# A one-core hybrid encoder step: the last group's value tiles get a pool of their own

## The chip, the cores and the metric

The kernel runs on one core of a Trainium2 chip. The metric is the device time of one execution in microseconds (us); of several runs the median counts. Engines are named as in the profile: PE is TensorE, the matrix engine (PEld are its weight loads), DVE is VectorE, ACT is ScalarE, POOL is GpSimd, SP is SyncE, which here issues the DMAs. L450 means line 450 of the kernel before.

## The reference

One inference step of a single layer, for a prompt of 1024 frames and, beside it, 32 frames of a running stream. All numbers are float32.

```python
proj = xn @ w_in                       # xn: normalised frames, (1056, 1024); w_in: 1024 columns of
                                       # queries and keys and more, then values and output gates
q, k, v, log_a -> o_a, s_gla           # gated linear attention, 6 heads, per-key decay
q, k, v, log_f -> o_b, s_hg            # HGRN2, 5 heads
q, k, v, log_f, ig -> o_c, (C, n, m)   # stabilised mLSTM, 5 heads, after a causal convolution
o = head_rms_norm(o) * gate            # for each of the three
x = x + rms_norm(concat(o_a, o_b, o_c) @ w_out)
up = causal_dwconv(rms_norm(x) @ w_up)
x = x + rms_norm((gelu(gate_half) * value_half) @ w_down)
```

The lines are shortened; the recurrences run in blocks of 64 frames, and the final states are outputs too.

## The kernel before, in words

The frames are cut into nine units: 0 to 7 are 128 prompt frames each, unit 8 is the 32 running frames. The in-projection works on three groups of units: 0 to 2, 3 to 5, and 6, 7 with 8 (288 frames). Its products are float32 built from three products of split operands: every operand x is kept as a rounded part xh and a rest xl, and a helper (`mm3`, L99 to L102) issues the three matmuls. Splitting costs a cast on ACT (sometimes on DVE) and a subtraction on DVE or POOL.

For each group the in-projection first makes the projections that feed queries, keys and gates (tiles `pf`), with their convolutions, exponentials and cumulative sums in the pool `pf`; the results go to DRAM (`qkb_d`, `mqk_d` and others) and are read back by the mixers. The last of them are four convolutions (`conv`, tiles pc, y, th, mo), whose results mo are stored to `mqk_d` and `mqks_d`. Then come eight blocks of 256 columns of values and output gates. In the first two groups, and for block 0, frames are the rows of the result. In the last group blocks 1 to 7 are computed the other way round (`vg_across`, L438): for each half e of a block, 24 matmuls put 128 columns by 288 frames into a PSUM buffer pv, ACT copies that into half of a tile vf (L456), and PE transposes vf back, unit by unit, into another PSUM buffer pb (`back`, L440 to L445). The transposes of a block are issued behind the matmuls of the next. From pb a value block goes through one ACT copy into a tile vg and out to DRAM; a gate block (blocks 4 to 7) goes through a tanh on ACT into a tile vth, of which there is one buffer, one or two DVE operations, and a product on POOL into vg (L408 to L424). Those PSUM buffers pv and pb, the transposes ctp and the products zp of the out-projection all have the tag "big" with three buffers.

The mixers (the three recurrences) are a generator per unit, 17 steps each, run in the order 0 to 5, then 8, 6, 7. They are traced between the steps of the in-projection of the next group and of the out-projection (`merge`, L1429).

The out-projection (`outproj`, L992) runs over the units 0, 1, 2, 3, 8, 4, 5, then 6 and 7. For a unit it loads the mixed frames ct from DRAM, transposes them on PE (ctp), splits them into ch (ACT, L1019) and cl (DVE, L1020), and multiplies with the eight slices of the split weights woh and wol, in two halves of 512 columns (zp). The weights are read from DRAM raw, slice by slice, into a ring of seven buffers wor that later holds ct, xr and z too (L664 to L669); slice 6 and 7 need a buffer that has been given back. `out_weights` (L979) splits the slices: the first two with ACT (L106) and DVE (L109), the others behind ch and cl of unit 0 (L986, L988).

On-chip memory is taken in pools that stack up from two sides. On the right, p1 holds the in-projection's tiles: x with the tag "x" (three buffers of 4 KB a partition, shared by the input frames and, in the last group, vf), gx, raw and split weights (tags wr, wh, wl), xh, xl, jk. p1 is closed after the three groups (L1455), and p2 (woh, wol, gm, ch, cl, oss) and p3 (x0, called xg in the profile) are opened in its place. On the left, above the mixers' pool mx, lies pf; in the last group it is closed after the convolutions, and pw, the ring of weights, is opened in its place (L662 to L664).

No order of the engines' instructions is written out here. A planner simulates a timeline and puts the instructions of each engine in order by priority, which follows the order of the trace except where `high_priority` or `issue_after` says otherwise. Waits between engines follow from the tiles' uses and from the pools. A pool that lands on a closed pool's bytes waits, by the default setting, for the users of that closed pool.

Of the kernel before, what the change touches and what calls it, by code (L numbers as in the profile page):

```python
# [8 lines left out]
F32 = mybir.dt.float32  # L9
# [81 lines left out]
def body(ctx: ExitStack, tc: tile.TileContext, a: dict):  # L91
# [7 lines left out]
    def mm3(ps, lh, rh, first, last, **kw):  # L99
        pe.matmul(ps, lh[0], rh[0], start=first, stop=False, **kw)  # L100
        pe.matmul(ps, lh[0], rh[1], start=False, stop=False, **kw)  # L101
        return pe.matmul(ps, lh[1], rh[0], start=False, stop=last, **kw)  # L102
# [21 lines left out]
    p1 = p1s.enter_context(tc.tile_pool(name="p1", bufs=1, side="right"))  # L124
# [127 lines left out]
    cols_of, dcs_of = {}, {}  # L252
    HSET = (2, 0, 4, 5)
    VGD = (lambda b, h: b > 0, lambda b, h: True, lambda b, h: True)
    pws, wo_raw, ring = ExitStack(), [], []
    NRING, CT0 = 7, 6

    ct_of, xr_of, tail, xlate, mixed = {}, {}, [], {}, set()
# [2 lines left out]
    def load_cat(u):  # L261
        if u in ct_of:
            return
        while u not in mixed:
            pump(1)
        n = 128 if u < 8 else DEC
        ct_of[u] = ring[0](f"ct{u}")
        sp.dma_start(ct_of[u][:n], cat_d[128 * u:128 * u + n, :])
# [8 lines left out]
    def units_of(g):  # L277
        t0, pl, sl = GROUPS[g]
        us = [(t0 // 128 + i, 128 * i, 128) for i in range(pl // 128)]
        if sl:  # L280
            us.append((8, pl, sl))
        return us
# [69 lines left out]
    def inproj(g, xh, xl, normed, scaled=None):  # L352
        t0, pl, sl = GROUPS[g]
        T = pl + sl
# [43 lines left out]
        def vg_weights(blk):  # L398
            parts = [(a["w_tok0"][:, ks[0]:ks[-1] + 1], ks, lt0_d[:, ks[0]:ks[-1] + 1]) for ks in VG0] if not blk else \
                [(a["w_tok"][blk - 1, hf], range(4 * hf, 4 * hf + 4), lt_d[blk - 1, hf]) for hf in range(2)]  # L400
            ws = []
            for i, (src, ks, low) in enumerate(parts):
                wh, wl, _ = weights(src, p1, f"wt{g}_{blk}_{i}", [128, len(ks), 256 if blk else 282],
                                    raw=wraw.pop((blk, i), None), eng=dve if VGD[g](blk, i) else pool, low=low, kept=g > 0)
                ws += [(wh[:, k], wl[:, k]) for k in range(len(ks))]
            return ws

        def vg_store(blk, u, off, n, ps):  # L408
            o = mx.tile([128, 256], F32, tag="vg", name=f"vg{u}_{blk}", bufs=3)
            t = t0 + off  # L410
            if blk < 4:
                act.copy(o[:n], ps[:n, :256])
                sp.dma_start(v_d[t:t + n, 256 * blk:256 * blk + 256], o[:n])
                return
            c0 = 256 * (blk - 4)
            th = mx.tile([128, 256], F32, tag="vth", name=f"vth{u}_{blk}", bufs=1)
            tanh(th[:n], ps[:n, :256], 0.5)
            ns = min(max(704 - c0, 0), 256)
            if ns:
                dve.scalar_tensor_tensor(th[:n, :ns], th[:n, :ns], 1.0, ps[:n, :ns], op0=ALU.add, op1=ALU.mult)  # L420
            if ns < 256:
                dve.tensor_scalar(th[:n, ns:], th[:n, ns:], 1.0, None, op0=ALU.add)
            pool.tensor_tensor(o[:n], th[:n], gh[:n, c0:c0 + 256], op=ALU.mult)
            sp.dma_start(g_d[t:t + n, c0:c0 + 256], o[:n])  # L424
# [13 lines left out]
        def vg_across(blks):  # L438

            def back(blk, fs, part):  # L440
                for (u, off, n) in units_of(g)[part]:
                    ps = psb.tile([128, 256], F32, tag="big", name=f"pb{u}_{blk}")
                    for e in range(2):
                        pe.transpose(ps[:n, 128 * e:128 * e + 128], fs[e][:, off:off + n], ident)
                    vg_store(blk, u, off, n, ps)  # L445

            before = None
            for blk in blks:
                ws = vg_weights(blk)
                fs = p1.tile([128, 2, T], F32, tag="x", name=f"vf{blk}", bufs=3)  # L450
                fs = [fs[:, 0], fs[:, 1]]
                for e in range(2):
                    ps = psb.tile([128, T], F32, tag="big", name=f"pv{g}_{blk}_{e}")
                    for k in range(8):
                        mm3(ps, [w[:, 128 * e:128 * e + 128] for w in ws[k]], (xh[:, k, :], xl[:, k, :]), k == 0, k == 7)
                    act.copy(fs[e], ps)  # L456
                    if before:
                        back(*before, slice(e, 1 + 2 * e))
                    yield
                before = (blk, fs)  # L460
                yield
            for e in range(2):
                back(*before, slice(e, 1 + 2 * e))
# [197 lines left out]
        if g == 2:  # L661
            pfs.close()  # L662
            pw = pws.enter_context(tc.tile_pool(name="pw", bufs=1, side="left"))
            ring.append(lambda name: pw.tile([128, 1024], F32, tag="ring", name=name, bufs=NRING))  # L664
            for k in range(8):
                if k == CT0:
                    load_cat(0)
                wo_raw.append(ring[0](f"wor{k}"))
                sp.dma_start(wo_raw[k], a["w_out"][k])  # L669
        if sl:  # L670
            yield from vg_across(range(1, 8))
            return
# [746 lines left out]
    side = []  # L1419
# [17 lines left out]
    def mixers(g):  # L1437
        us = [(u, 2 * i) for i, (u, off, n) in enumerate(units_of(g))]
        return chain_of(*[mixer(u, g, c) for (u, c) in us[-1:] + us[:-1]]) if us[-1][0] == 8 else \
            chain_of(*[mixer(u, g, c) for (u, c) in us])  # L1440
# [3 lines left out]
    for g in range(3):  # L1444
        xs_ = norm_tiles(g)
        n_side = (0, 3 * NMIX - 6, 3 * NMIX)[g]
        scaled = scale_x(0) if g == 0 else None
        if scaled:
            next(scaled)
            next(scaled)  # L1450
        merge(inproj(g, *xs_, norm_group(g, *xs_), scaled), NIN, n_side)
        if g == 0:
            mixer_zeros()
        side.append(mixers(g))
    p1s.close()  # L1455
    p2s = ExitStack()
    p2 = p2s.enter_context(tc.tile_pool(name="p2", bufs=1, side="right"))
    wo = outproj_setup(p2)
# [42 lines left out]
    blk = up_block(pw_, 0, 0, W0, X[0], uus[0], own)  # L1501
# [184 lines left out]
```

## Time and profile before

| what | us |
|---|---|
| median of 3 runs | 1431.09 |
| lowest and highest of them | 1427.78 and 1431.60 |
| profiled execution, its own time | 1433.42 |
| its span, first to last instruction | 1431.6 |
| PE busy in the span | 1375.1 (96%) |
| DVE busy | 1006.9 (70%) |
| ACT busy | 710.2 (50%) |
| POOL busy | 273.5 (19%) |

The times of instructions are counted from the span's start. A row of the timeline gives start, duration, engine, line, operation, the tiles written and read, shapes and the number of merged instructions; in brackets stands how long the engine was idle before it and what ended that. A row of waits names who waited for whom, then the total, the number and the longest. A row of the chain gives start, share on the chain, and the instruction. Matmuls are pipelined, so the durations of neighbours overlap.

In this execution the last group's value blocks run from 438.7 to 525.8, the out-projection's products zp from 536.0 to 701, and the feed-forward part fills the rest.

### The profile page before, as it was taken

The numbers are of one execution on the slowest core, as the hardware profiler recorded it, in microseconds if no ns is written. First come the engines' busy times: TensorE is split into PE (matmuls) and PEld (weight loads), VectorE is DVE, ScalarE is ACT, GpSimd is POOL, SyncE is SP. The second block draws the span as 40 slices with busy tenths as digits, with TensorE's granted clock in tenths as the row PEclk, the third lists the DMA queues.
The fourth block names the chain that finished last, engine by engine and source line by source line (L and its number), as shares of the span: only waits on it lengthen the run. The fifth ranks groups of instructions, "written<-read, shape, count | busy, mean of one in ns | idle before, by whom it ended". The sixth has DMA issues, their size and how long they took to land.

```text
span 1431.6 us, 30048 instructions
## 1 busy us (share of the span) xinstructions
PE 1375.1 (96%) x11804; PEld 1258.5 (88%) x11804; DVE 1006.9 (70%) x1827; ACT 710.2 (50%) x1403; POOL 273.5 (19%) x456
## 2 busy tenths in 40 slices
PE   7989999999998999899989999999999999999998
PEld 6989889898887887767789999999999999988886
DVE  5796468846597669685888887887888875653644
ACT  5545456535474546243665454554555455543432
POOL 6531111213021244132221111111111110000100
PEclk9999999999999999999999999999999999999999
DMA  9599778766789845352412222222222257775752
GB/s 345 189 317 355 229 244 298 236 228 210 262 248 303 313 124 188 122 178 60 162 54 91 85 82 91 75 78 73 91 75 75 76 183 235 227 230 180 238 180 99
DMA packets 132438, 255.11 MB, mean 178 GB/s; under 512 B 28648, under 2 KB 79368, under 8 KB 132296
## 3 DMA queue, kind: packets, MB, share of 16 engines
q1 hardware_dynamic: 132295, 253.19, 53.3%
q8 instruction: 92, 1.51, 0.4%
q14 instruction: 51, 0.41, 0.1%
HBM read 192.26 MB, written 60.89 MB: 177 GB/s over the span
## 4 chain that ended last, share of the span: by engine, by line
PE 71%; DVE 11%; DMA 8%; ACT 5%; issue 3%; POOL 2%; SPq 1%; DVEq 0%; POOLq 0%; ACTq 0%
PE pd L102 6%; PE pd L101 6%; PE pd L100 6%; PE pux L102 4%; PE pux L100 4%; PE pux L101 4%; PE pv L102 3%; PE pv L100 3%; PE pv L101 3%; PE puw L100 3%; PE puw L101 3%; PE puw L102 3%; DMA qkb<-qkb_d 2%; PE zp L100 2%; PE zp L101 2%
## 5 line engine op out<-in xcount | busy, mean ns | idle before, releaser
L1260 DVE SCALAR_TENSOR_TENSOR y<-uu,fconv_sb,y 128x1060 f32<-128x1060 f32 x88 | 116.3, 1321 | 28.3 <-ACT y L1258 27.5
L102 PE MATMUL pd<-wd,hl 128*128 128x512 f32 x264 | 105.1, 399 | 0.0
L101 PE MATMUL pd<-wd,hh 128*128 128x512 f32 x264 | 104.2, 395 | 0.0
L100 PE MATMUL pd<-wd,hh 128*128 128x512 f32 x264 | 103.5, 393 | 0.0
L1254 POOL COPY uu<-uu 128x2 f32<-128x2 f32 x44 | 35.3, 802 | 210.0 <-DVE uu L1202 209.9
L1197 ACT COPY c<-pux 128x274 f32<-128x274 f32 (+1 forms) x132 | 48.9, 375 | 41.2 <-PE pux L102 38.3
L1258 ACT ACTIVATE y<-uu,fconv_sb 128x1060 f32<-128x1060 f32 x44 | 56.0, 1273 | 21.1 <-POOL uu L1255 20.6
L100 PE MATMUL zp<-woh,ch 128*128 128x512 f32 (+1 forms) x144 | 58.8, 415 | 3.9 <-DVE cl L1020 2.9
L101 PEld LDWEIGHTS pd<-wd,hh 128*128 128x128 f32 x264 | 49.6, 188 | 12.5
L100 PEld LDWEIGHTS pd<-wd,hh 128*128 128x128 f32 x264 | 49.6, 188 | 11.7
L102 PEld LDWEIGHTS pd<-wd,hl 128*128 128x128 f32 x264 | 49.6, 188 | 11.4
L100 PE MATMUL pv<-wt_0h,xh 128*128 128x256 f32 (+2 forms) x195 | 57.8, 297 | 1.7 <-ACT xh L316 1.7
L101 PE MATMUL zp<-wol,ch 128*128 128x512 f32 (+1 forms) x144 | 58.8, 408 | 0.0
L102 PE MATMUL zp<-woh,cl 128*128 128x512 f32 (+1 forms) x144 | 58.2, 408 | 0.2 <-DVE cl L1020 0.2
L102 PE MATMUL pv<-wt_1h,xl 128*128 128x256 f32 (+2 forms) x195 | 57.4, 294 | 0.5 <-DVE xl L317 0.5
L102 PE MATMUL pv<-wt_0h,xl 128*128 128x256 f32 (+2 forms) x195 | 57.1, 293 | 0.6 <-DVE xl L317 0.6
L101 PE MATMUL pv<-wt_1l,xh 128*128 128x256 f32 (+2 forms) x195 | 56.9, 292 | 0.0
L100 PE MATMUL pv<-wt_1h,xh 128*128 128x256 f32 (+2 forms) x195 | 56.9, 292 | 0.0
L101 PE MATMUL pv<-wt_0l,xh 128*128 128x256 f32 (+2 forms) x195 | 56.8, 291 | 0.1
L100 PE MATMUL pd<-hh,wd 128*128 128x288 f32 x176 | 52.1, 297 | 0.0
L101 PE MATMUL pd<-hl,wd 128*128 128x288 f32 x176 | 52.1, 296 | 0.0
L218 POOL TENSOR_SCALAR hrs<-hss 128x5 f32<-128x5 f32 (+3 forms) x27 | 14.5, 537 | 196.4 <-DVE hss L888 195.8
(1675 smaller groups left out, 5179.5 us busy)
## 6 DMA issues: line engine op xcount, KB each, us to landing
h_d<-y SPq DMA_DIRECT2D x22, 530.0 KB, 3.3
wt_0r<-in_w_tok SPq DMA_DIRECT2D x21, 512.0 KB, 5.5
wt_1r<-in_w_tok SPq DMA_DIRECT2D x21, 512.0 KB, 5.9
wt_0l<-lt_d SPq DMA_DIRECT2D x14, 512.0 KB, 4.5
wt_1l<-lt_d SPq DMA_DIRECT2D x14, 512.0 KB, 5.6
qkb<-qkb_d SPq DMA_DIRECT2D x8, 768.0 KB, 6.4
hr<-h_d SPq DMA_DIRECT2D x44, 128.0 KB, 3.3
hr<-h_d SPq DMA_DIRECT2D x22, 192.0 KB, 4.1
```

The source lines that it names most:

```text
L100: pe.matmul(ps, lh[0], rh[0], start=first, stop=False, **kw)
L101: pe.matmul(ps, lh[0], rh[1], start=False, stop=False, **kw)
L102: return pe.matmul(ps, lh[1], rh[0], start=False, stop=last, **kw)
L218: pool.tensor_scalar(out, ss, 1.0 / width, EPS, op0=ALU.mult, op1=ALU.add)
L1197: kept[name] = act.copy(t, ps)
L1254: pool.tensor_copy(u[:, GAP_P:GAP_P + 2], u[:, GAP_S - 2:GAP_S])
L1258: act.activation(y, u, AF.Identity, scale=fconv[:, j, 2:3], bias=fconv[:, j, 3:4])
L1260: dve.scalar_tensor_tensor(y, uu[i][:, s:s + NCOL], fconv[:, j, s:s + 1], y, op0=ALU.mult, op1=ALU.add)
```

## The change

The tiles vf leave the tag "x" of p1. They get a pool of their own, pvf, with three buffers of 2,304 bytes a partition, opened on the left right after pw (so above it, on bytes that pf had) and closed right after p1, before p2 is opened. Everything else, each instruction and each DMA, is the same.

```diff
@@ body
-    pws, wo_raw, ring = ExitStack(), [], []
+    pws, pvs, wo_raw, ring, vfs = ExitStack(), ExitStack(), [], [], []
@@ vg_across
                 ws = vg_weights(blk)
-                fs = p1.tile([128, 2, T], F32, tag="x", name=f"vf{blk}", bufs=3)
+                fs = vfs[0].tile([128, 2, T], F32, tag="vf", name=f"vf{blk}", bufs=3)
                 fs = [fs[:, 0], fs[:, 1]]
@@ inproj
         if g == 2:
             pfs.close()
             pw = pws.enter_context(tc.tile_pool(name="pw", bufs=1, side="left"))
+
+            vfs.append(pvs.enter_context(tc.tile_pool(name="pvf", bufs=1, side="left")))
             ring.append(lambda name: pw.tile([128, 1024], F32, tag="ring", name=name, bufs=NRING))
@@ body, after the three groups
     p1s.close()
+    pvs.close()
     p2s = ExitStack()
```

## The prediction

> **What bounds the kernel now.** I read the page first, then the busy time by stretches, then the waits on the two tiles that the change separates, then the timeline at both ends of their life. The page gives the frame:
>
> ```profile
> span 1431.6 us, 30048 instructions
> PE 1375.1 (96%) x11804; PEld 1258.5 (88%) x11804; DVE 1006.9 (70%) x1827; ACT 710.2 (50%) x1403; POOL 273.5 (19%) x456
> ```
>
> PE (TensorE) is busy for 96% of the span, so a change can only win where PE idles or runs slowly. The next view gives, for each stretch, busy time and count of PE, weight loads, DVE, ACT and POOL, then the granted clock, the DMA share and GB/s.
>
> ```profile
> 456.00:460.00 4.00, 2.29 (x18) 2.04 (x16) 2.63 (x6) 3.01 (x9) 0.00 (x0) 1.00 0.87 317
> 460.00:464.00 4.00, 2.42 (x13) 2.43 (x14) 3.80 (x12) 1.82 (x4) 0.00 (x0) 0.79 1.01 399
> 464.00:526.00 62.00, 61.60 (x816) 55.69 (x815) 37.96 (x119) 29.81 (x79) 20.06 (x25) 0.99 0.68 233
> 526.00:532.00 6.00, 5.59 (x101) 3.95 (x100) 3.51 (x12) 1.85 (x5) 2.04 (x4) 0.88 0.15 49
> 532.00:536.00 4.00, 3.30 (x22) 2.45 (x20) 3.52 (x6) 2.20 (x4) 0.22 (x1) 0.50 0.90 269
> 536.00:541.00 5.00, 5.00 (x13) 3.94 (x13) 4.43 (x12) 4.80 (x7) 0.73 (x1) 0.52 0.95 317
> 551.00:576.00 25.00, 21.25 (x212) 16.35 (x211) 23.10 (x51) 14.82 (x38) 14.07 (x16) 0.98 0.44 143
> 576.00:582.00 6.00, 6.00 (x15) 4.71 (x16) 3.79 (x8) 1.15 (x2) 0.74 (x2) 0.52 0.65 225
> ```
>
> Three readings. From 464 to 526, the value blocks of the last group, PE has no holes: what is lost before 464 stays lost. From 526 to 541, the seam between the projections, few matmuls run and the granted clock falls to half. From 551 to 576 DVE is the full engine (23.10 of 25), so an out-projection tile that ends early gains only if DVE's work comes early too.
>
> The wait that the change aims at, in the timeline of the seam. PE's last value product, its last transpose, and the way to the first product of the out-projection:
>
> ```profile
> 525.45 0.30 PE L102 MATMUL pv<-xh,wt_1l 128*128 128x288 f32 x1
> ...
> 530.73 0.61 PE L444 MATMUL pb<-ident,vf 128*32 128x128 f32 x2
> ```
>
> ```profile
> 534.21 0.91 PE L692 MATMUL mi<-vm,kw 32*64 32x65 f32 x10 [0.70 <-DVE kw L922]
> 535.05 1.12 PE L1016 MATMUL ctp<-ident,ct 128*128 128x128 f32 x4
> 535.99 0.76 PE L100 MATMUL zp<-woh,ch 128*128 128x512 f32 x1
> ```
>
> The same time on ACT, on DVE, and on POOL and the DMA queue:
>
> ```profile
> 530.47 0.38 ACT L112 ACTIVATE vth<-pb 128x256 f32<-128x256 f32 x1 [1.91 <-POOL vg L423]
> 531.37 1.99 ACT L106 CAST woh<-wor 128x1024 fp32r<-128x1024 f32 x2 [0.52 <-PE pb L444]
> 533.33 0.58 ACT L1019 CAST ch<-ctp 128x512 fp32r<-128x512 f32 x1
> 533.81 0.39 ACT L112 ACTIVATE vth<-pb 128x256 f32<-128x256 f32 x1
> ```
>
> ```profile
> 532.82 1.20 DVE L109 TENSOR_TENSOR wol<-wor,woh 128x1024 fp32r<-128x1024 f32 x1
> 533.95 0.20 DVE L922 TENSOR_TENSOR kw<-mi,cols 32x64 f32<-32x64 f32 x1
> 534.08 1.20 DVE L109 TENSOR_TENSOR wol<-wor,woh 128x1024 fp32r<-128x1024 f32 x1
> 535.22 0.67 DVE L1020 TENSOR_TENSOR cl<-ctp,ch 128x512 fp32r<-128x512 f32 x1
> ```
>
> ```profile
> 531.40 0.11 POOL L1466 MEMSET xg<- 128x16 f32 x1 [0.96 <-PE pb L444]
> 531.40 0.33 SPq L976 DMA_DIRECT2D gm<-in_grows x1
> ```
>
> Three tiles of the pools opened after the in-projection's pool p1 (woh, gm, xg), on three engines, start within 0.03 us of each other, just behind the last transpose pb of a vf tile. So a pool waits for every user of the pool it replaces, whatever bytes its tile has. Without vf, p1's last users are the matmuls pv, whose last starts at 525.45 and lasts 0.30.
>
> **The change part by part.** No instruction, byte or DMA is added or removed: 14 copies into vf and their transposes stay. Two waits move.
>
> *The end: p2 opens earlier.* p2 holds woh and wol (32 KB a partition each), gm (4), ch and cl (6 each): 80 KB. p1 holds x, wr (12 each), gx (4), wh, wl (16 each), xh, xl (12 each) and jk (2): 86 KB. So p2 lies on p1 alone, and it opens at 525.45 + 0.30 = 525.75 instead of 531.37: 5.6 us earlier. That is the most the start of the out-projection can gain directly. How much arrives follows from what is late next. The two casts of woh (1.99) and two subtractions into wol (2 x 1.20) move into 526 to 531, where the rows above leave ACT 4.1 of 6 us and DVE 2.5 of 6 free, so they cost nothing there as long as they do not push the mixer's short DVE steps. But the first product zp also needs ch and cl, thus the transposes ctp, thus a PSUM buffer of the three called "big". Those are held by the last transposed value blocks, and each drains through one vth buffer: ACT tanh, DVE, POOL, and only then the next tanh (the rows at 530.47 and 533.81). This chain does not start from p2. What the new opening surely removes is the wol subtraction at 532.82, which stands before kw (533.95), which PE's mi, ctp and zp wait behind: the second transposed mi is written by 533.22 + 0.29, so kw, and with it ctp and zp, come 533.95 − 533.51 = 0.4 us earlier. At most the subtractions' two places ahead of cl also go: ch is done at 533.91, so cl can start there rather than at 535.22, 1.3 us. Likewise the tanh at 533.81 no longer stands behind the casts.
>
> ```profile
> 533.22 0.29 PE L692 MATMUL mi<-ident,mqk 64*32 64x64 f32 x1
> ```
>
> Then the last two weight slices: their loads wait for ring buffers that the first two splits free, and ACT waits for them:
>
> ```profile
> 543.48 1.05 ACT L986 CAST woh<-wor 128x1024 fp32r<-128x1024 f32 x1 [1.70 <-DMA wor<-in_w_out]
> ```
>
> With the buffers free some 5 us earlier the 1.70 us goes; how much of it PE would see no row says, so I count none. I take 1.5 us for this end: the 0.4 that is sure plus most of the 1.3. It is nearer to the lower bound because the rows name another late thing directly behind each removed one. Bounds: 0 and 5.6, and with the half clock, below, 8.2.
>
> *The start: vf now waits for pf.* The new pool pvf is opened on the left, above pw, on bytes of the closed pool pf (pw takes 28 KB; fr 6, e 12, q 3, pc, mo 3 each and the rows make pf some 38 KB). By the same rule its first tile waits for every user of pf. Which user is last, pw shows today:
>
> ```profile
> SPq L669 <- DMA mqk_d<-mo: 4.8, 1, 4.8
> ```
>
> ```profile
> 447.16 0.38 ACT L456 COPY vf<-pv 128x288 f32<-128x288 f32 x1
> 448.04 1.05 ACT L332 CAST wt_0h<-wt_0r 128x1024 fp32r<-128x1024 f32 x1 [0.49 <-PE pv L101]
> 456.99 0.63 ACT L743 ACTIVATE eb<-qkb 128x512 f32<-128x512 f32 x1 [7.91 <-DMA qkb<-qkb_d]
> ...
> 461.14 0.68 ACT L456 COPY vf<-pv 128x288 f32<-128x288 f32 x2
> ```
>
> ```profile
> 457.50 2.73 SPq L669 DMA_DIRECT2D wor<-in_w_out x6
> ```
>
> ```profile
> 454.82 0.30 PE L100 MATMUL pv<-xh,wt_0h 128*128 128x288 f32 x1
> ...
> 458.02 0.27 PE L444 MATMUL pb<-ident,vf 128*128 128x128 f32 x1
> ...
> 461.58 0.33 PE L444 MATMUL pb<-ident,vf 128*128 128x128 f32 x1 [3.28 <-ACT vf L456]
> ```
>
> The first weight slice of pw leaves at 457.50, when the convolution's stores have landed. So the first copy into vf goes from 447.16 to about 457.3, 10 us later. ACT's queue is in order, but ACT waits for qkb until 456.99 anyway. PE's three "big" buffers still take the first block's two halves and the second block's first half, so PE reaches its present stall at 458.02 all the same. That stall ends when ACT has worked through its burst and made two more copies; now it has three to make: one copy more, 0.68 / 2 = 0.34 us, or with the cast of wt_0h queued behind the waiting copy 1.05 more. I take 0.7 us. Bounds: 0.3 and 4.3, the latter in the rival below; a gain is excluded, since nothing becomes ready earlier there. With no holes from 464 to 526, it is lost for good. SP's queue does not change: it already sits behind the same wait.
>
> *The order.* What a product zp costs at half and at full clock, from the chain of the seam:
>
> ```profile
> 537.60 0.43 PE zp L100
> ```
>
> ```profile
> 541.21 0.23 PE zp L102
> ```
>
> The instruction order comes from a planner that simulates the timeline, so both moved waits can reorder what follows from 447 on. The trace cannot show that. I price it by the largest single disturbance in the rows: from 576 to 582 PE ran 15 matmuls, nearly all zp, at half clock, 0.43 instead of 0.23 us each, 3.0 us, after 3.75 us of idling in 551 to 576; together 6.7. One such dip more or fewer is the bound, above and below; I take 0, since no row speaks for a sign.
>
> Sum: −1.5 + 0.7 = −0.8 us, of which later stages keep all, since the next ones are bound by DVE and PE work that follows in order. The profiled execution took 1433.4 us, its span 1431.6; the sum gives it 1432.6, and the median of the runs, 1431.1, becomes 1430.3. I say 1430. A difference of 0.3%, 4.3 us, is about what a measurement of this kernel can tell from no change.
>
> **The half clock in the seam.** From 532 to 541 the clock is at about 0.5, though PE's records fill 3.30 of 4 us: transposes and small mixer products. The 13 matmuls from 536 to 541, nearly all of them zp, cost 13 x (0.43 − 0.23) = 2.6 us too much. [...]
>
> **The rivals.** *Faster: the whole opening is used.* If the planner puts ctp before the last value transposes, zp starts near 531, 5 us earlier, and the dip, which the rows show only where dense products pause (0.99 from 464 to 526), may go as well: 5.6 + 2.6 − 0.7 = 7.5, hence 1424. Losing the dip at 576 instead gives −0.8 − 6.7, the same 1424. For it: DVE and ACT are half free in 526 to 532. Against it: the PSUM buffers and the vth chain.
>
> *Slower: the copy of vf takes the place of the wait removed.* If the planner leaves the first copy ahead of the cast of wt_0h, ACT holds that cast until 457.6, the second block starts at 458.7 instead of 454.8, and ACT's burst ends 1.7 us later. PE then idles 4 us from 454.7 and may run its next 5 us at half clock (2.6 us, as in 536 to 541): 4.3 us; with nothing gained at the end, 1435.4, and one disturbance in the order takes it to 1438. It decides from a PE loss of 5.8 us, which eats the 1.5 and 4.3 more. For it: the DMA share is 0.87 to 1.01 there, so the landing can slip. Against it: ACT idles there now.
>
> *The change doesn't do what it says.* PSUM buffers alone pace the seam; only the 0.7 is left: 1431.8. This is within the 0.3%.
>
> **How the numbers follow.** My forecast, with the null rival in it, is a time within 0.3%: 0.40. The faster rival has 0.32, for the freed 5.6 us are real and lie where PE is poorly fed. The slower one has 0.28: the new wait is certain, and its size depends on an order I cannot see. The range reaches to 1423, the whole opening and a little more, and to 1437, the slower rival with most of a dip; about one in ten lies beyond on each side. Forecast alone: 1427 to 1435.
>
> **What would show it.** In the profile after: woh's first cast near 526 and no longer behind pb; gm and xg at a different time from the cast, xg still behind vf if its pool reaches pvf's bytes; the first vf copy at about 457, released by a DMA of mo; the first zp between 534 and 535.5; the wait for wor gone. I am wrong if zp starts before 532, if PE's hole at 456 to 464 grows by over 2 us, or if a half-clock stretch appears or vanishes after 540.

## The result, and the profile after

The changed kernel takes 1437.33 us (median of 8 runs, 1435.07 to 1440.17), beside 1429.35 us for the kernel before (8 runs, 1427.35 to 1434.54). The ratio is 1.0053, 95% interval 1.0039 to 1.0066: 0.5% slower, some 8 us. In a second set of runs (a1) the same kernel came out at 1.0057 (1.0035 to 1.0080). The forecast was 1430, no change, in a range of 1423 to 1437; the time lies 0.3 us beyond its upper edge and 7 us from the forecast. One execution of the kernel before, of 5847 us, is left out of all that follows.

The profiled execution of the changed kernel took 1436.48 us. That is 3 us over the profiled execution of the kernel before, not 8, because the latter (1433.42) was 4 us over the median of its kernel. One pair of traces is therefore not enough here, and the section after next uses all runs.

The page of the changed kernel, its span and its engines' line:

```profile
span 1434.7 us, 30059 instructions
...
PE 1376.7 (96%) x11804; PEld 1259.8 (88%) x11804; DVE 1009.2 (70%) x1827; ACT 712.0 (50%) x1403; POOL 269.4 (19%) x456
```

The same stretches as in the prediction (busy time and count of PE, weight loads, DVE, ACT, POOL; then granted clock, DMA share, GB/s), changed kernel:

```profile
456.00:460.00 4.00, 0.78 (x5) 0.47 (x5) 3.51 (x11) 3.91 (x11) 0.00 (x0) 1.00 0.90 323
460.00:464.00 4.00, 4.00 (x21) 3.69 (x21) 3.96 (x11) 1.63 (x6) 1.49 (x2) 0.65 1.04 420
464.00:526.00 62.00, 60.58 (x803) 54.50 (x803) 37.31 (x114) 27.61 (x73) 18.78 (x24) 1.00 0.62 219
526.00:532.00 6.00, 3.94 (x70) 2.84 (x68) 4.57 (x10) 2.75 (x5) 0.72 (x1) 0.79 0.52 183
532.00:536.00 4.00, 4.00 (x39) 3.46 (x36) 1.21 (x5) 0.97 (x3) 1.44 (x2) 0.50 0.60 194
536.00:541.00 5.00, 5.00 (x21) 4.02 (x19) 3.57 (x12) 3.66 (x6) 1.57 (x3) 0.63 0.68 216
...
551.00:576.00 25.00, 23.80 (x221) 17.82 (x220) 20.54 (x46) 14.88 (x37) 11.15 (x14) 1.00 0.31 92
576.00:582.00 6.00, 5.80 (x25) 4.80 (x26) 5.38 (x14) 1.59 (x3) 1.29 (x2) 1.00 0.49 160
```

At the start no clear loss shows: PE is busy for 0.78 + 4.00 = 4.78 us of 456 to 464, where it was 4.71 before. Fewer matmuls fall into it (26 against 31), with a granted clock of 0.65 against 0.79 from 460 to 464, and the last pv starts 0.70 us later (526.15 against 525.45); but in a1, the same kernel again, it starts at 525.33. The seam is worse: from 526 to 532, where p2 is now open, DVE has more work (4.57 against 3.51) and PE less (3.94 against 5.59). The half-clock stretch at 576 is gone, which did not make the kernel faster: in this execution three others, of 3.4 us each, begin at 594.3, 638.7 and 679.6, where the kernel before ran at full clock.

The timeline of the changed kernel at both ends, first ACT at the start, then PE, ACT, DVE, POOL and the DMA queue at the seam (start, duration, engine, line, operation; in brackets the idle time before it and what ended it):

```profile
454.79 0.64 ACT L745 ACTIVATE eb<-qkb 128x512 f32<-128x512 f32 x1 [10.45 <-DMA qkb<-qkb_d]
...
456.50 0.37 ACT L456 COPY vf<-pv 128x288 f32<-128x288 f32 x1
...
526.15 0.30 PE L102 MATMUL pv<-xh,wt_1l 128*128 128x288 f32 x1
...
529.58 0.63 PE L694 MATMUL sc<-Qz,qkb 64*32 64x32 f32 x16 [1.38 <-DVE P L784]
530.89 0.69 PE L444 MATMUL pb<-ident,vf 128*128 128x128 f32 x2 [0.68 <-DVE vth L420]
...
535.40 0.61 PE L444 MATMUL pb<-ident,vf 128*32 128x128 f32 x2
...
538.35 0.80 PE L100 MATMUL zp<-woh,ch 128*128 128x512 f32 x1
...
526.78 1.99 ACT L106 CAST woh<-wor 128x1024 fp32r<-128x1024 f32 x2
528.67 0.39 ACT L112 ACTIVATE vth<-pb 128x256 f32<-128x256 f32 x1
...
538.67 5.78 ACT L988 CAST woh<-wor 128x1024 fp32r<-128x1024 f32 x6
...
527.86 1.23 DVE L109 TENSOR_TENSOR wol<-wor,woh 128x1024 fp32r<-128x1024 f32 x1 [0.24 <-ACT woh L106]
529.00 0.52 DVE L784 COPY_PREDICATED P<-masks_sb,sc 32x176 f32<-32x176 int32 x1
529.34 1.24 DVE L109 TENSOR_TENSOR wol<-wor,woh 128x1024 fp32r<-128x1024 f32 x1
530.50 0.33 DVE L420 SCALAR_TENSOR_TENSOR vth<-vth,pb 128x192 f32<-128x192 f32 x1
...
531.07 0.72 POOL L423 TENSOR_TENSOR vg<-vth,gh 128x256 f32<-128x256 f32 x1 [6.65 <-DVE vth L422]
...
536.07 0.11 POOL L1469 MEMSET xg<- 128x16 f32 x1 [1.00 <-PE pb L444]
...
526.51 0.33 SPq L978 DMA_DIRECT2D gm<-in_grows x1
```

The waits moved as the change means them to: the casts of woh start at 526.78 (531.37 before) and gm leaves at 526.51, both right behind the last pv at 526.15, while xg still waits for the last pb. But the first zp comes at 538.35, 12.2 us behind the last pv instead of 10.5. The rows show what stands in the way. ACT casts woh for 1.99 us ahead of a tanh, and DVE has two subtractions of 1.23 and 1.24 us ahead of that tile's next step, which starts at 530.50. PE waits 1.38 us for a short copy into P that stands between the two subtractions, and then 0.68 us for that step on vth before the next pb at 530.89. POOL starts its product at 531.07, and the last pb comes at 535.40. With the casts put back (b3, below) the first zp is 10.2 us behind the last pv again.

**A second loss, elsewhere.** The planner's new order also changed how two small products of the mixers, om and oi, stand on PE. In the timeline of the kernel before they come in runs:

```profile
508.50 0.79 PE L692 MATMUL om<-vm,w 64*64 64x65 f32 x18
...
512.35 0.64 PE L692 MATMUL oi<-C,mqz 128*64 128x65 f32 x16
```

In the changed kernel they take turns:

```profile
510.24 0.33 PE L694 MATMUL oi<-C,mqz 128*64 128x65 f32 x2
510.50 0.33 PE L694 MATMUL om<-vm,w 64*64 64x65 f32 x2
510.75 0.33 PE L694 MATMUL oi<-C,mqz 128*64 128x65 f32 x2
511.01 0.33 PE L694 MATMUL om<-vm,w 64*64 64x65 f32 x2
```

A run of 16 takes 0.64 us, 0.04 us each, so two take 0.08; two between turns start 0.26 us after the two before them. A turn between tiles of 64*64 and of 128*64 thus costs 0.26 − 0.08 = 0.18 us here. What PE does in that time the rows do not show.

### The profile page after: what moved, and what is told of

Its sections match the earlier page's. It is cut to its first block, busy times and chain, and to the rows that moved or that the text cites. A ratio compares the mean times of both kernels' runs of the same rounds, so it can differ in the third digit from the quotient of the medians.

```text
span 1434.7 us, 30059 instructions
## 1 busy us (share of the span) xinstructions
PE 1376.7 (96%) x11804; PEld 1259.8 (88%) x11804; DVE 1009.2 (70%) x1827; ACT 712.0 (50%) x1403; POOL 269.4 (19%) x456
## 4 chain that ended last, share of the span: by engine, by line
PE 76%; DVE 9%; DMA 4%; ACT 4%; issue 3%; POOL 2%; SPq 1%; POOLq 0%; DVEq 0%; ACTq 0%
PE pd L102 6%; PE pd L101 6%; PE pd L100 6%; PE pux L100 4%; PE pux L102 4%; PE pux L101 4%; PE pv L102 3%; PE pv L100 3%; PE pv L101 3%; PE puw L100 3%; PE puw L101 3%; PE puw L102 3%; PE mi L694 2%; PE pf L100 2%; PE pf L102 2%
## 5 line engine op out<-in xcount | busy, mean ns | idle before, releaser
L1256 POOL COPY uu<-uu 128x2 f32<-128x2 f32 x44 | 30.7, 697 | 209.7 <-DVE uu L1204 209.5
```

The lines of the kernel that those rows point to most:

```text
L1256: pool.tensor_copy(u[:, GAP_P:GAP_P + 2], u[:, GAP_S - 2:GAP_S])
```

## The experiments

**How the runs are read.** Each run is listed with its span and its mean granted clock. In the traces of the kernel before and of the changed one the granted clock stands at 1.00 or at 0.50. Span x (1 − clock) is the time lost to the half clock; span x clock is the rest, roughly the time that the work in its order would take at full clock. This is a way of counting: half-clock time in which PE waited for another engine counts as lost too. The means over all runs of a kernel (in us, with their standard errors):

```
kernel                              turns  casts of woh  time     ratio [95%]             rest          lost to the clock
before (four chips, 113 runs)         37   late          1429.0-1430.6  1                 1405.1-1405.8  21.7-23.3
changed                               57   early         1437.33  1.0053 [1.0039,1.0066]  1410.3 ± 1.0   25.3 ± 1.2
changed, again (a1)                   57   early         1437.87  1.0057 [1.0035,1.0080]  1411.5 ± 0.9   24.6 ± 1.6
changed, pool waits by tile (a4)      57   early         1436.81  1.0063 [1.0039,1.0088]  1411.2 ± 0.4   25.0 ± 1.6
pool for blocks 1-4 alone (a2)        41   late          1434.69  1.0029 [1.0011,1.0047]  1409.7 ± 0.6   23.2 ± 1.0
pool for blocks 5-7 alone (a3)        53   early         1436.38  1.0037 [1.0018,1.0056]  1408.4 ± 0.5   25.0 ± 1.2
changed, casts put back (b3)          41   late          1437.12  1.0047 [1.0030,1.0064]  1409.5 ± 1.1   25.4 ± 1.7
before, turns forced (b4)             89   late          1432.20  1.0021 [1.0010,1.0032]  1412.8 ± 0.8   18.0 ± 0.8
blocks 1-4, eb behind vf (c1)         45   late          1432.90  1.0024 [1.0011,1.0037]  1408.8 ± 0.8   22.3 ± 1.1
changed, casts back, eb behind (c2)   45   late          1434.60  1.0033 [1.0019,1.0047]  1407.8 ± 0.7   24.8 ± 1.0
before, no turns (b1)                 17   late          1424.01  0.9956 [0.9941,0.9972]  1401.0 ± 0.9   21.7 ± 0.7
before, no turns, again (d3)          17   late          1424.59  0.9959 [0.9945,0.9974]  1403.3 ± 0.8   19.0 ± 1.2
before, no turns, other way (c4)      17   late          1425.02  0.9973 [0.9955,0.9990]  1402.0 ± 0.6   21.6 ± 0.8
changed, no turns (b2)                17   early         1429.82  0.9999 [0.9988,1.0010]  1402.7 ± 0.6   25.5 ± 0.7
changed, no turns, again (d4)         17   early         1428.08  0.9992 [0.9981,1.0004]  1402.3 ± 0.8   24.4 ± 0.8
changed, no turns, eb behind (d1)     17   early         1429.43  0.9997 [0.9985,1.0009]  1400.5 ± 0.6   26.8 ± 0.8
changed, no turns, casts back (d2)    17   late          1423.82  0.9961 [0.9948,0.9975]  1404.1 ± 1.2   18.3 ± 1.3
changed, no turns, both back (c3)     17   late          1424.45  0.9963 [0.9947,0.9979]  1403.3 ± 0.8   19.6 ± 0.9
```

"Turns" counts how often the names om and oi change places in the order written for PE, over the whole program (17 with none inside a unit). "Early" casts stand ahead of four tanh steps of the last value blocks on ACT, "late" ones behind the first tanh of block 7, where the kernel before has them. Each ratio is to the kernel before in runs on the same chip.

**The two halves of the change (a1 to a4).** Two of these take the pool for a part of the blocks only and leave x for the others; one lets the pool's tiles wait by tile, so that the written order is that of the change but the first vf copy has no wait for the stores of the convolution.

```diff
-                fs = vfs[0].tile([128, 2, T], F32, tag="vf", name=f"vf{blk}", bufs=3)
+                fs = (vfs[0].tile([128, 2, T], F32, tag="vf", name=f"vf{blk}", bufs=3) if blk < 5 else p1.tile([128, 2, T], F32, tag="x", name=f"vf{blk}", bufs=3))
```

In a3 the condition is `blk > 4`. In a4:

```diff
-            vfs.append(pvs.enter_context(tc.tile_pool(name="pvf", bufs=1, side="left")))
+            vfs.append(pvs.enter_context(tc.tile_pool(name="pvf", bufs=1, side="left", reuse_waits="tile")))
```

> The changed kernel once more, with its lines kept at the numbers of the kernel before. It should take 0.3 to 0.7% more than the kernel before (about 1437 against 1429 us), with the first zp some 6 to 8 us after the last pv of the in-projection's value blocks has ended plus what is lost before, and it gives a second trace to tell what belongs to the change and what to one execution.

> Value blocks 1 to 4 use the new pool, blocks 5 to 7 the old tag x. So the first copy of vf waits for pf as in the change, and the out-projection's pool opens behind the last transposes as before. Theory 'start' (the new wait of vf on pf and the order the planner makes of it are the loss): slower than before by 2 to 5 us. Theory 'end' (the early splits of the weights get in the way of the last value blocks): same as before within 1.5 us.

> Value blocks 1 to 4 use the old tag x, blocks 5 to 7 the new pool. So the first copy of vf does not wait for pf, and the out-projection's pool opens early as in the change. Theory 'end' (splits of woh and wol stand ahead of tanh, DVE and POOL steps that drain the last value blocks): slower than before by 3 to 7 us, first cast of woh within 1 us of the last pv, last pb 4 us later than in the kernel before. Theory 'start': same as before or up to 4 us faster, since the opening is gained and nothing is lost before.

> The changed kernel with the same order of instructions on every engine, but its new pool waits tile by tile, so that the first copy of vf does not wait for the stores of pf. If the wait itself costs: 2 to 3 us faster than the change. If only the order that the planner made costs: the same as the change within 1 us.

Both halves cost on their own, 0.29% and 0.37%, so neither is the gain that the other one eats. In a1 the first zp comes 12.2 us behind the last pv, as in the first trace, and not the 6 to 8 that I expected. The wait itself costs nothing: without it the change takes as long (1436.81), the first copy being where its place behind eb and qe puts it (in its trace eb at 451.84, qe at 452.38, the copy at 453.54). What is left as the main suspect is the order that the planner writes once the waits are in its simulated timeline.

**Turns (b1, b2, b4, c4).** oi of a unit is put behind its last om (b1, b2), om behind its last oi (c4), or the two are made to take turns head by head (b4).

```diff
+        for h in range(5):
+            for ch, (o, m) in enumerate(chunks):
+                last = first(pe.matmul, om[o:o + m, h, :], ..., start=True, stop=True)
         for h in range(5):
             for ch, (o, m) in enumerate(chunks):
-                first(pe.matmul, oi[o:o + m, h, :], ..., start=True, stop=True)
+                with tc.issue_after(last.ins): first(pe.matmul, oi[o:o + m, h, :], ..., start=True, stop=True)
```

> The kernel before, with the oi matmuls of a unit of the mixer put behind its last om matmul on PE, so that the two shapes of tile (64*64 and 128*64) no longer take turns; in the written order of PE the two names change places 17 times in the whole program instead of 37 (57 in the changed kernel). Theory (taking turns costs PE time: in the out-projection om and oi took 2.6 us more in the changed kernel than before, and 1.0 us more ahead of it, for 20 more turns, so some 0.15 to 0.18 us a turn): 20 turns less are worth 3.0 to 3.6 us, so about 1426 us where the kernel before takes 1429.5. Rival (the longer start-to-start times only use up gaps that PE has anyway): 1428.5 to 1430.5, no change. A second rival: the fixed order makes PE wait for operands of om, so slower than before, 1431 or more.

> The changed kernel, with the oi matmuls of a unit behind its last om matmul; 17 turns instead of 57. Theory: 40 turns at 0.15 us are 6 us, and what is left is the late first zp (1.7 us) and the rest of the stretch behind the first vf copy (some 1.5 us): about 1431.5 to 1433 us. Rival (turns fill gaps): 1436 to 1438, as the changed kernel. If the first zp stands as far behind the last pv as in the changed kernel (12.2 us) while the span from first to last zp falls by 2.5 us, the turns and the early splits are two separate losses.

> The kernel before, with oi and om of each unit made to take turns head by head on PE: 89 turns instead of 37. Theory: 52 turns at 0.15 us are 7.8 us, so about 1437 us. Rival (turns fill gaps): 1429 to 1431. If the time grows, but the start-to-start time of om and oi does not, the price is that of waiting in a fixed order and not of the turns.

> The kernel before with the turns taken away the other way round: the om matmuls of a unit behind its last oi matmul, 17 turns as with the first way. Theory (the number of turns is what counts): 1423 to 1425.5, as the first way (1424.0). Rival (the first way gained because oi, which is written first, waited less or let other work ahead): 1427 to 1430.

Taking the turns away makes both kernels faster: the kernel before by 0.44% and 0.41%, and by 0.27% (0.10 to 0.45) with om behind oi; the changed kernel by about 8 us, to the time of the kernel before. The groups of om and oi of the 128-frame units (columns: busy us, mean ns of one, idle before) show where. Kernel before, changed kernel, kernel before without turns, kernel before with turns forced:

```profile
L692 PE MATMUL oi<-C,mqz 128*64 128x65 f32 x160 | 12.5, 235 | 1.1 <-DVE cat L890 0.9 <-DVE C L935 0.2
L692 PE MATMUL om<-vm,w 64*64 64x65 f32 x160 | 10.4, 229 | 0.4 <-DVE w L912 0.4
```

```profile
L694 PE MATMUL oi<-C,mqz 128*64 128x65 f32 x160 | 14.0, 233 | 1.7 <-DVE C L937 1.4 <-DVE cat L892 0.3
L694 PE MATMUL om<-vm,w 64*64 64x65 f32 x160 | 12.2, 229 | 0.0
```

```profile
L692 PE MATMUL oi<-C,mqz 128*64 128x65 f32 x160 | 9.0, 227 | 0.3 <-DVE C L935 0.3
L692 PE MATMUL om<-vm,w 64*64 64x65 f32 x160 | 8.0, 232 | 0.6 <-DVE w L912 0.6
```

```profile
L692 PE MATMUL oi<-C,mqz 128*64 128x65 f32 x160 | 16.0, 246 | 1.0 <-DVE C L935 0.6 <-DVE cat L890 0.4
L692 PE MATMUL om<-vm,w 64*64 64x65 f32 x160 | 13.6, 243 | 0.0
```

Busy time is 22.9, 26.2, 17.0 and 29.6 us for 37, 57, 17 and 89 turns. With the turns forced the rest grows by 7.5 us for 52 turns, 0.14 us each, near the 0.15 expected; the time grows by only 3, because that kernel also lost 5 us less to the half clock, which I did not expect and cannot explain. b1 and b2 came out some 2 us below what I expected, b4 some 5. Without turns the rest falls by 4.3 (b1), 2.4 (d3) and 3.8 (c4) against the kernel before on the same chip, for 20 turns: 0.22, 0.12 and 0.19 each. By 0.12 to 0.22 us, the 20 turns that the change adds are 2.4 to 4.4 us of the 5 to 6 us by which its rest is longer. The edit that removes the turns removes all of it: 1402.7, 1402.3 and 1400.5 for the changed kernel against 1401.0, 1403.3 and 1402.0. That edit moves other matmuls too, so what lies beyond the price of the turns, 1 to 4 us, stays unassigned.

The count of turns is not the whole account. Kernels a2 and b3 have 41 turns, 4 more than the kernel before, and yet 4 us more rest (1409.7 and 1409.5). Part of the remainder may lie in other products: counted over all matmuls of the traces, PE changes its tile shape 415 times in the kernel before, 440 in the changed one, 397 in b1 and 465 in b4. At 0.12 to 0.22 us the 25 more of the change would be 3 to 5.5 us; but a2 has only 422 and b3 424, so their 4 us are not explained by this count either.

**The casts put back (b3, d2), the start put back (c1, d1), and both (c2, c3).** The casts:

```diff
-            tanh(th[:n], ps[:n, :256], 0.5)
+            held.append((blk, act.activation(th[:n], ps[:n, :256], AF.Tanh, scale=0.5)))
...
-                split(W[1][:, k, :], W[2][:, k, :], wo_raw[k], dve)
+                with tc.issue_after(held[-3][1].ins): split(W[1][:, k, :], W[2][:, k, :], wo_raw[k], dve)
```

The start, with the pool's waits by tile as in a4:

```diff
-                    act.copy(fs[e], ps)
+                    vfc.append(act.copy(fs[e], ps))
...
-        act.activation(ebf, b4.rearrange("p f n -> p (f n)"), AF.Exp)
+        with tc.issue_after(vfc[0].ins) if vfc and u == 5 else ExitStack(): act.activation(ebf, ..., AF.Exp)
```

> The changed kernel, with the first two casts of woh put behind the first tanh of value block 7 on ACT, which is where the kernel before has them. Nothing else is given. Theory (the early casts and subtractions push the tanh, DVE and POOL steps that drain the last value blocks): the first zp comes 10.5 us behind the last pv as before and not 12.2, the last pb 4 us earlier; the planner also returns to 41 turns of om and oi from 57. Both together: some 3 to 4 us off, 1433 to 1434.5, which is the time of the run with only the first blocks in the pool (1434.7). Rival (the drain is set by the wait for the vth buffer and POOL, whatever ACT does first): 1436 to 1438.

> The kernel with value blocks 1 to 4 in the pool, with two things besides: the pool's tiles wait by tile (so the first vf copy does not wait for the stores that read the memory it lies on), and the eb of unit 5 is put behind that copy on ACT. The written order is then that of the kernel before but for 14 rows of ACT and 66 of PE, with 45 turns of om and oi instead of 41 (37 before). Where the span is split by each run's mean granted clock into a part lost to the clock and the rest, the kernel before has 1405.1 us of rest, and the run with blocks 1 to 4 in the pool 1409.7. Theory (the planner's order behind the late vf copy costs, not the pool): rest 1405.5 to 1407, time 1429.5 to 1431.5. Rival (the pool costs wherever its copies stand, by its place in memory or by its own waits for three buffers): rest 1409 to 1410.5, time 1434 to 1435.

> The changed kernel with both orders put back by hand: waits by tile in the pool and the eb of unit 5 behind the first vf copy, and the first two casts of woh behind the first tanh of block 7; 45 turns of om and oi. Theory: rest 1406 to 1407.5 (8 turns over the kernel before at 0.15 to 0.2 us), time 1430 to 1432.5: the moved waits are worth nothing once the order is as it was. Rival (the early opening of the second part costs by itself, through more half clock or through the transfers that it starts): as the changed kernel with only the casts put back, rest 1409.5, time 1435 to 1437.

> The same with the oi matmuls of a unit behind its last om matmul, 17 turns. Theory: as the kernel before with that same edit, rest 1400.5 to 1402, time 1423.5 to 1425.5. Rival (grouped, the changed kernel still lost 1.7 us of rest and 3.7 us of clock to the grouped kernel before, 1429.8 against 1424.0; if that is the pool and not the order, it stays): 1428.5 to 1430.5.

b3 missed: its trace shows the first zp 10.2 us behind the last pv again, but its time, from six runs spread over 8 us, is that of the change. c1 did not do what it was for. Its timeline on ACT:

```profile
456.24 1.28 ACT L788 ACTIVATE qe<-qkb,cf_sb 128x128 f32<-128x128 f32 x4 [7.11 <-DMA qkb<-qkb_d]
457.43 0.37 ACT L456 COPY vf<-pv 128x288 f32<-128x288 f32 x1
```

eb went behind the copy, but qe, which waits for the same load, came ahead of it, so the copy stayed 10 us late (447.16 in the kernel before). c1, c2 and d1 are therefore runs with another order at the start, not with the old one. c2, with 45 turns and the casts put back, still takes 1434.60 (1.0033), between what the theory and the rival expected. c3, with no turns, both edits in it and the late copy still there, equals the kernel before without turns (1424.45 against 1424.01 and 1424.59). That pointed to the orders and not the pool, and left open which of them costs the 6 us between b1 and b2. One more set, all without turns and on one chip:

> The changed kernel without turns of om and oi, with the start's order put back (waits by tile in the pool, eb of unit 5 behind the first vf copy); the two early woh casts stay early. Theory (the order behind the late vf copy is the other loss, the early casts are not one): 1424 to 1426, rest 1401 to 1403.5. Rival (the early casts are the other loss): 1428.5 to 1430.5.

> The changed kernel without turns, with the two woh casts put back behind the first tanh of block 7; the first vf copy stays late. Theory: 1428.5 to 1430.5, as the changed kernel without turns (1429.8). Rival (the early casts are the loss, by the clock if not by the work): 1424 to 1426. If both this and the run with the start put back lie near 1427, the loss is shared.

> The kernel before without turns, once more, as the lower end on this chip: 1423 to 1425 by both theories.

> The changed kernel without turns, once more, as the upper end on this chip: 1428.5 to 1430.5 by both theories; if it comes out below 1427, the 5 us between the two grouped kernels were a chance of one chip and nothing but the turns is left to explain.

My theory fell and its rival held: with the casts put back and the copy of vf still late the kernel takes 1423.82, the kernel before 1424.59; with the casts early 1428.08 and 1429.43. So without turns the early casts are the whole loss, 4 to 6 us, and the late first copy costs nothing. The rest is not larger with early casts (1400.5 to 1402.7, against 1401.0 to 1404.1). It is the clock: 24.4 to 26.8 us lost, against 18.3 to 21.7.

The traces show the place. Twenty us from the last pv (the columns as in the stretches above; granted clock third from the end), in d3, the kernel before without turns:

```profile
515.13:535.13 20.00, 18.89 (x174) 13.92 (x173) 14.93 (x34) 11.98 (x19) 3.34 (x6) 0.83 0.72 244
```

in d2, with the casts put back:

```profile
517.74:537.74 20.00, 18.89 (x166) 14.04 (x164) 15.11 (x33) 11.21 (x17) 3.00 (x5) 0.74 0.66 220
```

in d4, with early casts:

```profile
517.35:537.35 20.00, 17.95 (x156) 13.57 (x155) 14.24 (x33) 10.93 (x16) 3.72 (x6) 0.66 0.69 212
```

and in d1, early casts too:

```profile
518.20:538.20 20.00, 17.76 (x155) 13.36 (x153) 14.23 (x33) 10.93 (x16) 3.72 (x6) 0.66 0.66 211
```

PE is busy 0.9 to 1.1 us less and the clock is 0.66 instead of 0.83 or 0.74. The timelines of the seam say what PE waits for. d4:

```profile
517.97 1.99 ACT L106 CAST woh<-wor 128x1024 fp32r<-128x1024 f32 x2
...
519.05 1.23 DVE L109 TENSOR_TENSOR wol<-wor,woh 128x1024 fp32r<-128x1024 f32 x1 [0.23 <-ACT woh L106]
520.20 0.52 DVE L784 COPY_PREDICATED P<-masks_sb,sc 32x176 f32<-32x176 int32 x1
...
520.77 0.63 PE L694 MATMUL sc<-Qz,qkb 64*32 64x32 f32 x16 [1.37 <-DVE P L784]
522.08 0.69 PE L444 MATMUL pb<-ident,vf 128*128 128x128 f32 x2 [0.68 <-DVE vth L420]
...
530.50 0.79 PE L100 MATMUL zp<-woh,ch 128*128 128x512 f32 x1
```

and d2:

```profile
519.15 0.33 DVE L420 SCALAR_TENSOR_TENSOR vth<-vth,pb 128x192 f32<-128x192 f32 x1
...
520.44 0.44 PE L694 MATMUL sc<-Qz,qkb 64*32 64x32 f32 x16 [0.27 <-DVE P L784]
...
528.54 0.76 PE L100 MATMUL zp<-woh,ch 128*128 128x512 f32 x1
```

In d4 the subtraction stands between PE's small product and the short DVE copy into P that the next one needs, and PE waits 1.37 us for it instead of 0.27; then the pb waits 0.68 for the tanh's DVE step. The first zp is 13.2 us behind the last pv, in d2 10.8. So the dense products begin later, and the half clock lasts longer: 13.65 us in d4, 10.24 in d2.

What 20 us at 0.83, 0.74 and 0.66 lose is 3.4, 5.2 and 6.8 us: steps of about 1.7. The granted clock in the traces has the same steps: at the seam it stands at half for 13.65 us without a break in d1, d4 and b2, for 10.24 in d2 and 6.83 in d3, four, three and two times 3.41, and 3.41 us at 0.50 lose 1.7. So in these traces the early casts (d1, d4, b2) come with one stretch of 3.41 us more than the casts put back (d2), and with two more than the kernel before without turns (d3). How long a delay has to be to bring one more, no run shows. In the profiled executions of the kernel before and of the changed one, both with turns, it is 10.24 us in each, so there this loss does not show.

## Why the prediction was wrong

- **The frame, right.** PE bounds the kernel (busy for 96% of the span before and after), a pool waits for all users of the one it replaces, p2 opens at the last pv (526.78 for the first cast, "near 526"), the first vf copy goes to "about 457" (456.50, though behind eb and qe and not behind a store of mo), xg stays behind vf, gm moves.
- **"They cost nothing there as long as they do not push the mixer's short DVE steps": the first step that failed.** The condition was named and then taken as met, from the free share of DVE in 526 to 532 (2.5 of 6 us). Free share is not a free place, and the rows above also show that cl, from whose place the 1.3 us was taken, is not read by the first zp (zp<-woh,ch) but only by later ones. What happened: the two subtractions fell between a PE product and the copy into P that the next one needs, and ahead of the tanh's DVE step. The 0.4 us that was called sure and the 1.3 became a first zp 1.7 us further from the last pv, at 538.35 where 534 to 535.5 was forecast. Without turns this costs 4 to 6 us, by the clock; with the turns in place, putting the casts back (b3) did not show in the time, so how much of the 8 us it carries is not shown.
- **"The order. I take 0, since no row speaks for a sign": the second, and the larger one.** The price was bounded at 6.7 by a half-clock dip at 576. The dip did vanish (three shorter ones came further on), but the order cost in another currency: 20 more turns of om and oi, 2.4 to 4.4 us, in a rest that grew by 5 to 6 us in all. That term belonged in the sum: with 0 in its place the forecast was 7 us too low. That a change of order costs up to 6.7 us either way was a guess from one dip, so that 1430.3 + 6.7 comes near the measured time is luck.
- **The start, mis-sized but harmless.** 0.7 us were counted and PE's busy time in 456 to 464 did not fall (4.71, now 4.78); without the wait the change takes as long. The half of the change with the start alone was 0.29% slower, and what in its order costs this is not shown; without turns nothing of it is left.
- **The slower rival, right in its time by luck and wrong in its mechanism.** 1435.4 to 1438 was forecast (its 1438 leaves out most of the disturbance priced at 6.7: 1435.4 + 6.7 is 1442.1) for an ACT that holds the cast of wt_0h behind the late copy. The planner put the copy behind eb and qe, the cast stayed ahead, and what the runs show of the loss lies in the order.
- **The wait for wor, right.** The six casts of woh behind ch now run from 538.67 without a stop (5.78 us for six); no gain from it shows in the time.

What stays open: the 1 to 4 us of rest beyond the price of the turns, and the 4 us of a2, which has only 4 turns more; why, with 41 turns and the casts put back, b3 returned 1 to 2 us of rest and none of the clock (25.4 ± 1.7); and why forced turns lose less to the clock.

The edit that beats both kernels is the one on the turns alone: the kernel before with oi behind the last om, 0.9956 (0.9941 to 0.9972) and again 0.9959 (0.9945 to 0.9974). The pool of its own adds nothing to it (0.9961 and 0.9963 with the casts put back).

## What to carry to other kernels

Where a planner writes the order, a wait that is moved is first of all a new order: look at what the early work lands in front of on each engine, and hold it back where a short step feeds PE (here this paid once the turns were gone). Keep small products of different tile shapes in runs on PE (here 64*64 and 128*64, for 0.27 to 0.44% of the time). When the clock steps (here between 1.00 and 0.50), compare kernels over all runs, split by the granted clock, before believing one trace.

## What the runs showed of the hardware

- A turn between matmuls of 64*64 and of 128*64 cost 0.18 us in the timeline of the changed kernel and, by the difference of the rest, 0.12 to 0.22 us a turn over whole runs (b1, d3, c4; 0.14 in b4).
- The half clock took 18 to 27 us, counted as above, on the mean of these kernels; single executions of the kernel before lost 16 to 30 us, beside times that spread over 12 us.
- In the traces of the kernel before and of the changed one the half clock came in stretches of 3.41, 6.83 and 10.24 us, the one at the span's end aside; at the seam it lasted 6.83, 10.24 or 13.65 us in the traces without turns.
- With 89 turns instead of 37 the same work lost 18.0 us to the clock instead of 23.2, so more than half of the 7.5 us that the turns added to the rest was given back. Which property of the order does this was not tried.
